# Hybrid linear-attention decode step: the gate's second product and the delta heads' decode update as float32r in row blocks of 32, another evacuation order for q and k, and packed last stores

## The chip, the cores and the metric

The kernel runs on one core of a Trainium2 chip. The metric is device time in microseconds (us): 997.32 us is the median of three runs (997.32, 997.32, 997.81). Five engines work side by side, each in its own order: PE (TensorE: matmuls; its weight loads are listed apart as PEld), DVE (VectorE), ACT (ScalarE), POOL (GpSimd) and SP, which here only issues DMAs. PE's granted clock was 0.997 of full speed in the profiled execution.

## The reference, cut to what matters

1024 prompt tokens and 8 x 8 sample tokens (T = 1088 in all) pass one layer, whose mixer has two linear-attention branches.

```python
proj = rms_norm(x) @ w_in         # q_a k_a v_a g_a z_a | qkv_b a_b b_b z_b | gate_a gate_b
# branch a (GLA, 4 heads of 64): a key-wise decay of low rank (16), from g_a
gk = log_sigmoid(g_a @ w_gla_gate + b_gla_gate) / 16
# S_t = diag(exp(gk_t)) S_{t-1} + k_t^T v_t ;  o_t = q_t S_t
# branch b (gated DeltaNet, 4 heads of 128): conv, SiLU, L2-normalised q and k, then
# S_t = exp(g_t)(I - beta_t k_t k_t^T) S_{t-1} + beta_t k_t v_t^T ;  o_t = q_t S_t
# in chunks: the inverse of (I + strict_lower(beta k k^T * gamma)) gives v_new, and
s = s * d_c + k_c^T @ v_new
# both branches: rms_norm(o) * silu(z) @ w_up, merged by sigmoid gates, @ w_out, residual,
# per-layer embedding gated by sigmoid(h @ w_ple_gate), final rms_norm
```

The outputs are y for all tokens and the new states, for the prompt and for each of the 8 sample sequences. All inputs and outputs are float32.

## The kernel before

Tokens lie along the free dimension: activations are tiles of 128 channels by tokens, in three chunks of 384, 384 and 320 tokens. PE takes a matmul of two float32 operands in two passes (two records of one instruction, such as `x2` in the timeline). The kernel avoids this nearly everywhere by splitting a float32 operand into two float32r parts, `hi` (a rounded copy, made on ACT, as `xh` from `x` or `wh` from `wr`) and `lo` (the remainder, subtracted on DVE, `xl` or `wl`), and summing three float32r products, hi·hi, hi·lo and lo·hi, in PSUM. Line 290 of the program is that product; a product of an input block over a chunk is 24 such matmuls. `w_split` (L174, L175) makes the parts of a 512 KB weight block.

*The start* is written out in order by hand: ACT, DVE, POOL and PE keep the order of the code up to `in_order.close()`. Here the first q and k blocks (`inqa`, `inka`) and half of the `v` tiles are multiplied by rows that are not normalised yet, while the row scales (`rsx`, `x_rs`) are worked out; `qk_out` then scales q and k when it evacuates them (`qa` at L385, `ka` at L391, on DVE). `x_scale` and `x_split` make the normalised `xr` and its parts for the later blocks, `x_scale` and the subtraction of `x_split` (L281) on DVE. `dup_x` copies the parts of the 64 sample tokens twice (`dupl`, `duph`) for the ninth `v` tile. 

*The recurrences* run as side tasks (generators) between the matmuls of the large input blocks. `sd.tick()` gives each a turn, and a `yield n` lets n turns pass. From the end of the written order on, a scheduler puts the instructions of each engine in order from what they need. So an edit in one task also moves instructions of others.

- `gates()` transposes the 16 gate columns `ga` of each of nine token tiles (128 columns each with zeros behind the 16) through PSUM into `gat`, evacuated on DVE (L458), and multiplies it by `wg` (16 rows of weights, zeros below) for two pairs of heads and three chunks: `gg`, L467, 6 float32 products of 128 rows. ACT and DVE turn `gg` into the running decay `b`, from which the factors `E` of the attention products `att` (L637) come.
- `gdn(h)` is the delta rule's chunked form for one head. `Gm` and `AT` are masks and products over 8 chunks. `B` holds 34 blocks of 32x32 that go through DRAM (`scra`, `scrb`), are inverted on DVE by 30 pairs of instructions `tm` (L953) and `B` (L955), and come back into `AT`; DVE transposes them into `X` (L972), and PE, ACT and DVE widen the inverses to 128 in four products (`z` L980, `x` L991 and on). Then 8 steps over the chunks (`ch`, L1034 to L1045) carry the state `S`, each passing between PE, DVE and ACT. Meanwhile the next head's convolution runs on DVE and ACT (`D`, L798).
- `gdn_sample(h)` does the same for the 64 sample tokens against 8 incoming states `S0b`. Its last step, the decode update, multiplies the keys `ktS` (32 tokens of 4 sequences at a time) by `vbb`, the new values `vn` spread over 4 sequences by a selection mask (DVE, L1122): `dSb`, L1131, two float32 products of 32 rows and 512 columns for each head. They are added to `S0b` (L1135) and stored (`out_gdn_s`, L1137). `lastpe` pins the first behind the last `ch` product so far.

*The end*: up products, output projection, the embedding's gate (`eg`, `ep`), and the final norm. The results of the last 256 tokens are made in two halves of 128 tokens and stored by four DMAs of 256 KB (`out_yT`, L1627). A partition's share of a DMA is four pieces of 128 tokens, each 512 B in DRAM.

Tiles named `half` (four slots of 128 partitions) hold, among others, `X`, `Z`, `S0b` and `vbb`; those named `small` hold `wg`, `ktS` and `vn`.

Of the kernel before, what the change touches and what calls it, by code (L numbers as in the profile page):

```python
# [104 lines left out]
def tile_hybrid_step(ctx: ExitStack, tc: tile.TileContext, xT, x0, pT, wqk, wmain, wv0, wv1, wup, wout, wpg, wpl, wgate,  # L105
                     pcols, rows, cst, sconv, sgla, sgdn,
                     yT, gla_p, gdn_p, conv_p, gla_s, gdn_s, conv_s):
    nc = tc.nc
# [40 lines left out]
    def ufree(n=1):  # L149
        sd.free_units += n  # L150
# [126 lines left out]

    def x_split(c):
        for k in range(8):
            A.copy(xh[c][:, k], xr[c][k])  # L280
            V.tensor_tensor(xl[c][:, k], xr[c][k], xh[c][:, k].bitcast(F32), op=ALU.subtract)  # L281
# [67 lines left out]
    load(rw, rows.broadcast_to([P, 8]))  # L349
    wg = [small(f"wg{hp}") for hp in range(2)]  # L350
    for hp in range(2):
        G.memset(wg[hp], 0.0)
        load(wg[hp][0:16, :], wgate[:, hp * P:(hp + 1) * P])
    K = kp.tile([P, C_K], F32, tag="K", name="K")
# [34 lines left out]
    def k_ev(hp, rs=None):  # L389
        if rs is not None:  # L390
            return lambda c, ps, o, w: V.tensor_tensor(ka[hp][:, o:o + w], ps[:, :w], rs, op=ALU.mult)  # L391
        return lambda c, ps, o, w: A.copy(ka[hp][:, o:o + w], ps[:, :w])

    def v_tiles(hf, whs, tts, dup, raw=False, lo_last=False):

        n = (272, 264)[hf]
        out = []
        for tt in tts:
# [23 lines left out]
            if hf == 0:  # L422
                A.copy(gas[tt // 4][:, (tt % 4) * P:(tt % 4) * P + 16], ps[:, 256:272])
            else:
                A.copy(ab[:, tt], ps[:, 256:264])
# [3 lines left out]
    def v_rows(tiles):  # L429
        for tt, ps in tiles:  # L430
            r = rsr[:, tt:tt + 1]
            A.mul(vr[0][tt // 4][:, (tt % 4) * 256:(tt % 4) * 256 + 256], ps[:, :256], r)
            A.mul(gas[tt // 4][:, (tt % 4) * P:(tt % 4) * P + 16], ps[:, 256:272], r)

# [12 lines left out]
    def gates():  # L447

        yield from sd.units(3)
        gat = unit("gat")  # L450
        for i in range(3):
            yield from sd.banks(1)
            n = 4 if i < 2 else 1
            ps = rps(f"gat{i}")
            for j in range(n):
                PE.transpose(ps[:, j * P:(j + 1) * P], gas[i][:, j * P:(j + 1) * P], ident)
            wd = n * P if i < 2 else NS
            V.tensor_copy(gat[:, i * 512:i * 512 + wd], ps[:, :wd])  # L458
            bfree()
            yield 5  # L460
# [409 lines left out]
    def gdn(h):  # L870
# [158 lines left out]
        for c in range(8):  # L1029
# [14 lines left out]
            mm(ps[:, 384:512], kt[:, s], vn, start=True, stop=True)  # L1044
            lastpe[h] = mm(ps[:, 0:P], Gm[:, s], vn, start=True, stop=True).ins  # L1045
            Sn = kp.tile([P, P], F32, tag="S", name=f"S{h}{c}", bufs=3)
# [40 lines left out]

    lastpe = {}

    def gdn_sample(h, kq_s, vtS, ktS, Cs, brk, sso, os_):  # L1090
# [15 lines left out]
        for b_ in range(4):  # L1106
            for c in range(4):
# [12 lines left out]
        bfree()  # L1120
        vb = half(f"vbb{h}")[lo, :512]
        V.tensor_tensor(vb.rearrange("p (b v) -> p b v", v=P), vn[lo].unsqueeze(1).broadcast_to([NS, 4, P]),  # L1122
                        sel4[lo].unsqueeze(2).broadcast_to([NS, 4, P]), op=ALU.mult)
        for g in range(2):
            V.tensor_tensor(S0v[g], S0v[g], sdec[:, h, 4 * g:4 * g + 4].unsqueeze(2).broadcast_to([P, 4, P]), op=ALU.mult)
        yield 4
        yield from sd.banks(2)
        pd = [rps(f"dSb{h}{g}") for g in range(2)]
        for g in range(2):
            r = slice(32 * g, 32 * g + 32)  # L1130
            e = mm(pd[g], ktS[r], vb[r], start=True, stop=True).ins  # L1131
            if g == 0 and h in lastpe:
                after(e, lastpe[h])
        for g in range(2):
            V.tensor_tensor(S0[g], S0[g], pd[g], op=ALU.add)  # L1135
            bfree()
# [460 lines left out]
    def normed(parts, pss, last, waits=0, ends=False):  # L1597
# [14 lines left out]
        for n, (c, r, *_) in enumerate(parts):  # L1612
            w, o, rs = r.stop - r.start, LCH[c][0] + r.start, rss[n]
            k = 4 if ends else 2
            for m0 in range(0, 8, k):
# [10 lines left out]
                yield waits  # L1626
                load(yT[m0:m0 + k, :, o:o + w].rearrange("m p w -> p m w"), yt)  # L1627

# [61 lines left out]
def _layout(i):  # L1690
# [16 lines left out]
    def vcols(m):  # L1707
# [8 lines left out]
    pcols = np.concatenate([cols(a["norm_w"]), cols(a["b_gla_gate"]), cols(a["gla_norm_w"]), cols(a["gdn_norm_w"]),  # L1716
                            cols(a["final_norm_w"]), convw], 1)
    return dict(
        xT=x.T.reshape(8, P, T), x0=x.T.reshape(8, P, T)[:, :, :384], pT=p.T.reshape(2, P, T), wqk=wqk, wmain=wmain, wv0=wv0, wv1=wv1,
        wup=np.concatenate([blocks(a["w_up_gla"][0]), blocks(a["w_up_gdn"][0])], 0)  # L1720
        .reshape(2, 2, 4, P, 4, P).transpose(0, 2, 3, 1, 4, 5).reshape(8, P, 8, P),
        wout=blocks(a["w_out"][0]), wpg=blocks(a["w_ple_gate"][0]), wpl=wpl, wgate=a["w_gla_gate"][0], pcols=pcols,
        rows=np.concatenate([a["gdn_a_log"], a["gdn_dt_bias"]], 1), cst=_consts(),
# [5 lines left out]

_OUTS = [("yT", (8, P, T)), ("gla_p", (2, P, P)), ("gdn_p", (4, P, P)), ("conv_p", (P, 12, 3)),  # L1730
         ("gla_s", (2, P, 8, P)), ("gdn_s", (4, P, 8, P)), ("conv_s", (P, 12, 24))]


def _results(g):
    y = g["yT"].reshape(1024, T).T
    return (
# [27 lines left out]
```

## Time and profile before

| | us |
|---|---|
| median of 3 runs | 997.32 |
| the profiled execution | 997.55 |
| its span (first to last instruction) | 995.4 |
| PE busy | 982.9 |
| weight load busy (beside PE) | 951.4 |
| DVE busy | 650.9 |
| ACT busy | 413.2 |
| POOL busy | 64.0 |

A row of the timeline holds the start in us from the beginning of the span, the duration in us (of all in the row), the engine, the line, the operation, `out<-in` by the program's names, the shapes, the count, and in brackets the idle time ahead of it with what ended it. Matmuls are pipelined and their ends are modelled, so starts are compared and not durations. A row of waits reads: who waited, `<-` for what, us in total, times, longest.

### The profile page before, as it was taken

What the parts mean: (1) busy time and instruction counts of PE and PEld (TensorE: products, weight loads), DVE (VectorE), ACT (ScalarE), POOL (GpSimd) and SP (SyncE); (2) the same over time, 40 slices, a digit from 0 to 9 for tenths busy, and PEclk for the clock granted to TensorE, in tenths of its full rate; (3) what the DMA queues carried; (4) which work ended last, traced back from release to release, by engine and by line L of the source; (5) the groups of instructions that cost most, each with busy time, mean ns of one, the idle gap of its engine ahead of it and who ended that gap; (6) DMA issues with size and microseconds to landing.
All of it is one profiled execution on the core that took longest, in us unless ns stands there. A gap on an engine that the chain in (4) does not pass through costs nothing.

```text
span 995.4 us, 17705 instructions
## 1 busy us (share of the span) xinstructions
PE 982.9 (99%) x6968; PEld 951.4 (96%) x6968; DVE 650.9 (65%) x1457; ACT 413.2 (42%) x989; POOL 64.0 (6%) x83
## 2 busy tenths in 40 slices
PE   9999999999999999999999999999999999999996
PEld 8999999999999989989999999999999999999996
DVE  6885745333847959866876785558777855853356
ACT  7764634432534524452264223235222222733354
POOL 0000011000000000010001000000000143200000
PEclk9999999999999999999999999999999999999998
DMA  8011112232222031313132222114442433421024
GB/s 315 15 43 64 49 57 72 77 88 72 96 73 71 30 102 23 100 66 78 68 98 73 56 77 89 43 46 141 141 126 89 132 102 89 150 85 43 22 93 152
DMA packets 65243, 84.74 MB, mean 85 GB/s; under 512 B 27188, under 2 KB 51192, under 8 KB 65160
## 3 DMA queue, kind: packets, MB, share of 16 engines
q1 hardware_dynamic: 64872, 83.22, 26.9%
q8 instruction: 55, 0.90, 0.4%
q10 hardware_dynamic: 288, 0.39, 0.1%
q14 instruction: 28, 0.23, 0.1%
HBM read 65.38 MB, written 18.21 MB: 84 GB/s over the span
## 4 chain that ended last, share of the span: by engine, by line
PE 56%; DVE 2%; ACT 0%; issue 0%; DVEq 0%
PE eg L290 10%; PE py L290 10%; PE s L1473 6%; PE inzb L290 5%; PE ing L290 5%; PE ingsg L290 5%; PE ingsh L290 4%; PE ep L290 2%; PE inza L290 1%; PE sf L1478 1%; PE se L1478 1%; PE ch L1040 1%; PE ch L1044 1%; PE ch L1045 1%; PE ch L1034 0%; PE ch L1035 0%
## 5 line engine op out<-in xcount | busy, mean ns | idle before, releaser
L175 DVE TENSOR_TENSOR wl<-wr,wh 128x1024 fp32r<-128x1024 f32 x59 | 71.9, 1221 | 65.1 <-ACT wh L174 64.7
L174 ACT CAST wh<-wr 128x1024 fp32r<-128x1024 f32 x59 | 61.7, 1049 | 107.1 <-PE ing L290 25.4
L290 PE MATMUL ing<-xh,wh 128*128 128x384 f32 (+1 forms) x288 | 97.1, 337 | 0.0
L290 PE MATMUL ing<-xh,wl 128*128 128x384 f32 (+1 forms) x288 | 94.8, 329 | 0.0
L290 PE MATMUL ing<-xl,wh 128*128 128x384 f32 (+1 forms) x288 | 94.6, 328 | 0.0
L290 PE MATMUL eg<-H,wh 128*128 128x416 f32 x256 | 69.3, 352 | 0.0
L290 PE MATMUL ingsg<-xh,wh 128*128 128x384 f32 (+1 forms) x192 | 66.5, 346 | 0.0
L290 PE MATMUL ingsh<-xh,wh 128*128 128x384 f32 (+1 forms) x192 | 66.2, 345 | 0.0
L290 PE MATMUL ingsg<-xl,wh 128*128 128x384 f32 (+1 forms) x192 | 63.1, 329 | 0.0
L290 PE MATMUL ingsh<-xl,wh 128*128 128x384 f32 (+1 forms) x192 | 62.9, 328 | 0.0
L290 PE MATMUL ingsg<-xh,wl 128*128 128x384 f32 (+1 forms) x192 | 62.8, 327 | 0.0
L290 PE MATMUL ingsh<-xh,wl 128*128 128x384 f32 (+1 forms) x192 | 62.8, 327 | 0.0
L290 PEld LDWEIGHTS ing<-xh,wh 128*128 128x128 f32 x288 | 54.2, 188 | 0.9 <-issue 0.7
L290 PEld LDWEIGHTS ing<-xl,wh 128*128 128x128 f32 x288 | 54.2, 188 | 0.5 <-issue 0.5
L290 PEld LDWEIGHTS ing<-xh,wl 128*128 128x128 f32 x288 | 54.1, 188 | 0.2 <-issue 0.2
L798 DVE SCALAR_TENSOR_TENSOR D<-R,cw,D 128x1112 f32<-128x1112 f32 x36 | 49.3, 1369 | 2.4 <-ACT D L796 2.2
L290 PEld LDWEIGHTS eg<-H,wh 128*128 128x128 f32 x256 | 47.7, 188 | 0.3
L290 PE MATMUL eg<-H,wl 128*128 128x416 f32 x128 | 44.5, 348 | 0.0
L953 DVE TENSOR_TENSOR tm<-B 34x30 f32<-34x30 f32 (+14 forms) x120 | 38.2, 319 | 7.4 <-DMA B<-scra 5.3
L955 DVE TENSOR_TENSOR B<-B,tm 34x30 f32<-34x30 f32 (+14 forms) x120 | 38.2, 318 | 1.8
L290 PEld LDWEIGHTS ingsg<-xh,wh 128*128 128x128 f32 x192 | 36.2, 188 | 2.2 <-issue 1.7
L290 PEld LDWEIGHTS ingsh<-xh,wh 128*128 128x128 f32 x192 | 36.2, 188 | 1.8 <-issue 1.1
(498 smaller groups left out, 2864.8 us busy)
## 6 DMA issues: line engine op xcount, KB each, us to landing
wr<-in_wmain SPq DMA_DIRECT2D x38, 512.0 KB, 3.5
wr<-in_wpg SPq DMA_DIRECT2D x13, 512.0 KB, 3.5
wr<-in_wup SPq DMA_DIRECT2D x8, 512.0 KB, 3.5
wr<-in_wout SPq DMA_DIRECT2D x8, 512.0 KB, 3.5
gt<-gscrg SPq DMA_DIRECT2D x16, 208.0 KB, 3.1
gt<-gscrh SPq DMA_DIRECT2D x16, 208.0 KB, 3.9
x<-in_xT SPq DMA_DIRECT2D x16, 208.0 KB, 2.4
out_yT<-y SPq DMA_DIRECT2D x8, 416.0 KB, 4.2
```

Of the source, the lines that this page charges most:

```text
L174: a = A.copy(wh, wr).ins
L175: b = (eng or V).tensor_tensor(wl, wr, wh.bitcast(F32), op=ALU.subtract).ins
L290: mm(ps[:, :w], l_, r_, start=i == 0, stop=i == len(seq) - 1)
L798: V.scalar_tensor_tensor(D[:, :n], R[:, i:n + i], cw[:, 4 * ci + i:4 * ci + i + 1], D[:, :n], op0=ALU.mult, op1=ALU.add)
L953: V.tensor_tensor(tv, Bv[:, j:j + 1, j + 1:32].broadcast_to([NBLK, j, n]), Bv[:, 0:j, j:j + 1].broadcast_to([NBLK, j, n]), op=ALU.mult)
L955: V.tensor_tensor(Bv[:, 0:j, j + 1:32], Bv[:, 0:j, j + 1:32], tv, op=ALU.add)
L1040: mm(ps[:, 256:384], AT[:, s], vt[:, s], start=True, stop=True)
L1044: mm(ps[:, 384:512], kt[:, s], vn, start=True, stop=True)
L1045: lastpe[h] = mm(ps[:, 0:P], Gm[:, s], vn, start=True, stop=True).ins
L1473: mm(ps, a[p_][:, k], Mp[b][k][q_], start=(k, i) == (0, 0), stop=(k, i) == (3, 2))
L1478: mm(ps, a[p_][:, k], M2[q_][:, k0 + k], start=first and (k, i) == (0, 0), stop=not first and (k, i) == (3, 2))
```

## The change

1. **The gate's second product.** Each 16 columns of `ga` are written four times, at 0, 32, 64 and 96, so that after the transposition the 16 rows stand in each of four row blocks of 32. ACT evacuates them as float32r, and DVE subtracts in rows 64 to 127, so that these hold the `lo` part. The weights are laid out likewise by the host (four blocks of 32 rows, 64 KB for each pair of heads rather than 8) and their blocks 1 and 3 become `lo`. One float32r product of 128 rows then sums hi·hi, hi·lo, lo·hi and lo·lo.
2. **The decode update.** A tile `kv` takes three row blocks of 32: keys as hi, hi and lo beside values as hi, lo and hi, made by 8 casts (ACT) and 4 subtractions (DVE) for each head. `vbb` is made twice, over 96 rows, and `dSb` is one float32r product of 96 rows for each half, one PSUM bank at a time. The pin `lastpe` is gone. The `half` tiles of a head are eight rather than six, in the same four slots.
3. **q and k ahead of x.** `x_split(1)` is cut in two, and the row scales and the evacuation of the third chunk's q and k stand ahead of its last three steps.
4. **Packed last results.** The four last stores go to an output of their own, `y2`, in which each partition's share (2 KB) is contiguous; the host puts it in place.

```diff
+    def gate_cols(tt):
+        return gas[tt // 4][:, (tt % 4) * P:(tt % 4) * P + P].rearrange("p (r n) -> p r n", n=32)[:, :, 0:16]
...
-                A.copy(gas[tt // 4][:, (tt % 4) * P:(tt % 4) * P + 16], ps[:, 256:272])
+                A.copy(gate_cols(tt), ps[:, 256:272].unsqueeze(1).broadcast_to([P, 4, 16]))
...
-        gat = unit("gat")
+        gat = unit("gat", F32R)
...
-            V.tensor_copy(gat[:, i * 512:i * 512 + wd], ps[:, :wd])
+            A.copy(gat[:, i * 512:i * 512 + wd], ps[:, :wd])
+            g_ = gat[NS:, i * 512:i * 512 + wd]
+            V.tensor_tensor(g_, ps[NS:, :wd], g_.bitcast(F32), op=ALU.subtract)
...
-            lastpe[h] = mm(ps[:, 0:P], Gm[:, s], vn, start=True, stop=True).ins
+            mm(ps[:, 0:P], Gm[:, s], vn, start=True, stop=True)
...
-        vb = half(f"vbb{h}")[lo, :512]
-        V.tensor_tensor(vb.rearrange("p (b v) -> p b v", v=P), vn[lo].unsqueeze(1).broadcast_to([NS, 4, P]),
-                        sel4[lo].unsqueeze(2).broadcast_to([NS, 4, P]), op=ALU.mult)
...
-        yield 4
-        yield from sd.banks(2)
-        pd = [rps(f"dSb{h}{g}") for g in range(2)]
+        kv = kp.tile([P, HW], F32R, tag="half", name=f"kv{h}", bufs=4)
+        kr, vr_ = (kv[:, o:o + 256].rearrange("p (g n) -> p g n", n=P) for o in (0, 256))
+        blk = [slice(32 * i, 32 * i + 32) for i in range(3)]
         for g in range(2):
-            r = slice(32 * g, 32 * g + 32)
-            e = mm(pd[g], ktS[r], vb[r], start=True, stop=True).ins
-            if g == 0 and h in lastpe:
-                after(e, lastpe[h])
+            me, other = blk[g], blk[1 - g]
+            for r in blk[:2]:
+                A.copy(kr[r, g], ktS[me])
+            for r in (me, blk[2]):
+                A.copy(vr_[r, g], vn[me])
+            V.tensor_tensor(kr[blk[2], g], ktS[me], kr[me, g].bitcast(F32), op=ALU.subtract)
+            V.tensor_tensor(vr_[other, g], vn[me], vr_[me, g].bitcast(F32), op=ALU.subtract)
+        yield 3
+        R3 = slice(0, 96)
         for g in range(2):
-            V.tensor_tensor(S0[g], S0[g], pd[g], op=ALU.add)
+            vb = kp.tile([P, HW], F32R, tag="half", name=f"vbb{h}{g}", bufs=4)[R3]
+            V.tensor_tensor(vb.rearrange("p (b v) -> p b v", v=P), vr_[R3, g].bitcast(F32).unsqueeze(1).broadcast_to([96, 4, P]),
+                            sel4[R3].unsqueeze(2).broadcast_to([96, 4, P]), op=ALU.mult)
+            yield 2
+            yield from sd.banks(1)
+            pd = rps(f"dSb{h}{g}")
+            mm(pd, kr[R3, g], vb, start=True, stop=True)
+            V.tensor_tensor(S0[g], S0[g], pd, op=ALU.add)
...
-    x_split(1)
-    ufree(5)
+    x_split(1, range(5))
     x_rs(2, ps)
     qk_out(2, evs)
+    x_split(1, range(5, 8))
+    ufree(5)
...
+    for w_, r_ in zip(wg, wgr):
+        A.copy(w_, r_)
+        for r in (slice(32, 64), slice(96, 128)):
+            V.tensor_tensor(w_[r], r_[r], w_[r].bitcast(F32), op=ALU.subtract)
...
-                load(yT[m0:m0 + k, :, o:o + w].rearrange("m p w -> p m w"), yt)
+                load(y2[r.start // w][:, m0:m0 + k] if ends else yT[m0:m0 + k, :, o:o + w].rearrange("m p w -> p m w"), yt)
```

In the rows below the word ahead of each is its line in the program, and the lines of the change are some 7 to 24 higher. The number behind a name tells apart tiles of one name.

The first place is DVE in the written order of the start, before: the scaling of the second chunk's x ends (`xl_388`), then q and k of the third chunk are evacuated.

```order
L281 TENSOR_TENSOR xl_388<-xr_118,xh_387 128x384 x2
L281 TENSOR_TENSOR xl_388<-xr_120,xh_387 128x384 x2
L281 TENSOR_TENSOR xl_388<-xr_122,xh_387 128x384 x2
L281 TENSOR_TENSOR xl_388<-xr_124,xh_387 128x384 x2
L385 SCALAR_TENSOR_TENSOR qa_193<-inqa_2_613,rsx_236 128x320
L391 TENSOR_TENSOR ka_194<-inka_2_638,rsx_236 128x320
L276 SCALAR_TENSOR_TENSOR xr_126<-xr_126,pc,rsx_236 128x320 x3
```

The same place after the change:

```order
L281 TENSOR_TENSOR xl_388<-xr_118,xh_387 128x384 x2
L281 TENSOR_TENSOR xl_388<-xr_120,xh_387 128x384 x2
L281 TENSOR_TENSOR xl_388<-xr_122,xh_387 128x384
L385 SCALAR_TENSOR_TENSOR qa_193<-inqa_2_613,rsx_236 128x320
L391 TENSOR_TENSOR ka_194<-inka_2_638,rsx_236 128x320
L281 TENSOR_TENSOR xl_388<-xr_122,xh_387 128x384
L281 TENSOR_TENSOR xl_388<-xr_124,xh_387 128x384 x2
L276 SCALAR_TENSOR_TENSOR xr_126<-xr_126,pc,rsx_236 128x320 x3
```

The two evacuations have moved ahead of three subtractions; nothing else has moved there.

The second place is PE in head 0's chunk steps, before: the pair of updates stands right behind the products of a `ch` step.

```order
L1040 MATMUL ch_4347<-R_3461,AT_2778 128x128
L290 MATMUL ing_0_4455<-xh_197,wl 128x384
L290 MATMUL ing_0_4455<-xh_197,wh 128x384
L290 MATMUL ing_0_4455<-xl_198,wh 128x384
L290 MATMUL ing_0_4455<-xh_197,wl 128x384
L1044 MATMUL ch_4347<-vn_4370,R_2627 128x128
L1045 MATMUL ch_4347<-vn_4370,Gm_2777 128x128
L1131 MATMUL dSb_4399<-vbb_4299,ktS_3052 128x512
L1131 MATMUL dSb_4400<-vbb_4299,ktS_3052 128x512
L1034 MATMUL ch_4415<-S_4387,D_2772 128x128
L1035 MATMUL ch_4415<-S_4387,D_2884 128x128
```

After the change, from the next step's first products on:

```order
L1041 MATMUL ch_4429<-S_4409,D_2781 128x128
L1042 MATMUL ch_4429<-S_4409,D_2893 128x128
L1150 MATMUL dSb_4444<-vbb_4398,kv_4310 128x512
L290 MATMUL ing_1_4527<-xl_388,wh 128x384
L290 MATMUL ing_1_4527<-xh_387,wl 128x384
L290 MATMUL ing_1_4527<-xh_387,wh 128x384
L290 MATMUL ing_1_4527<-xl_388,wh 128x384
L1047 MATMUL ch_4429<-R_3470,AT_2787 128x128
```

The first update stands behind the next step's first two products, alone between them and an in-block; the second follows 15 rows later, behind that step's last product and two in-block rows.

The third place is DVE at the end of head 1's inversion, before (rows of `B` and `tm` with other work between):

```order
L955 TENSOR_TENSOR B_3941<-B_3941,tm 34x26x5
L953 TENSOR_TENSOR tm<-B_3941 34x108
L955 TENSOR_TENSOR B_3941<-B_3941,tm 34x27x4
L953 TENSOR_TENSOR tm<-B_3941 34x84
L955 TENSOR_TENSOR B_3941<-B_3941,tm 34x28x3
L953 TENSOR_TENSOR tm<-B_3941 34x58
L955 TENSOR_TENSOR B_3941<-B_3941,tm 34x29x2
L175 TENSOR_TENSOR wl<-wr,wh 128x1024
```

After the change:

```order
L805 SCALAR_TENSOR_TENSOR D_4604<-R_4466,cw,D_4604 128x1112
L960 TENSOR_TENSOR tm<-B_3950 34x84
L805 SCALAR_TENSOR_TENSOR D_4604<-R_4466,cw,D_4604 128x1112
L962 TENSOR_TENSOR B_3950<-B_3950,tm 34x28x3
L805 SCALAR_TENSOR_TENSOR D_4604<-R_4466,cw,D_4604 128x1112
L960 TENSOR_TENSOR tm<-B_3950 34x58
L890 SCALAR_TENSOR_TENSOR Gm_4609<-Gm_4609,dcum,K 128x128
L962 TENSOR_TENSOR B_3950<-B_3950,tm 34x29x2
L890 SCALAR_TENSOR_TENSOR Gm_4609<-Gm_4609,dcum,K 128x128
L960 TENSOR_TENSOR tm<-B_3950 34x30
L890 SCALAR_TENSOR_TENSOR Gm_4609<-Gm_4609,dcum,K 128x128
L962 TENSOR_TENSOR B_3950<-B_3950,tm 34x30
```

Three convolution steps and three mask rows of the next head have come in between the last steps of the inversion, which before had them behind it. The rows that follow, up to the transposition into `X`:

```order
L890 SCALAR_TENSOR_TENSOR Gm_4609<-Gm_4609,dcum,K 128x128 x4
L894 SCALAR_TENSOR_TENSOR Gm_4609<-Gm_4609,dcum,K 64x64
L1085 TENSOR_SCALAR os_4022<-os_4022,rsto_4509 128x128
L175 TENSOR_TENSOR wl<-wr,wh 128x1024
L979 STREAM_TRANSPOSE X_4534<-AT_3498 32x8x32
```

Before, the weight split `wl` that stands here ahead of `X` stood behind it. And on PE the first of the sixteen pairs `z` of this head stood behind 14 matmuls of `ing_2`; now it stands behind all 24 of them and behind 15 of `ingsg_0`.

More of the change, by code (lines that the diff above doesn't have):

```diff
@@ L106, in tile_hybrid_step @@
                      pcols, rows, cst, sconv, sgla, sgdn,
-                     yT, gla_p, gdn_p, conv_p, gla_s, gdn_s, conv_s):
+                     yT, y2, gla_p, gdn_p, conv_p, gla_s, gdn_s, conv_s):
     nc = tc.nc
@@ L276, in x_scale, with x_split @@
             V.scalar_tensor_tensor(xr[c][k], xr[c][k], pc[:, V_NW + k:V_NW + k + 1], xs[c], op0=ALU.mult, op1=ALU.mult)
-    def x_split(c):
-        for k in range(8):
+    def x_split(c, ks=range(8)):
+        for k in ks:
             A.copy(xh[c][:, k], xr[c][k])
@@ L349, in tile_hybrid_step @@
     load(rw, rows.broadcast_to([P, 8]))
-    wg = [small(f"wg{hp}") for hp in range(2)]
+    wgr = [small(f"wgr{hp}") for hp in range(2)]
+    wg = [kp.tile([P, P], F32R, tag="sm", name=f"wg{hp}", bufs=13) for hp in range(2)]
     for hp in range(2):
-        G.memset(wg[hp], 0.0)
-        load(wg[hp][0:16, :], wgate[:, hp * P:(hp + 1) * P])
+        load(wgr[hp], wgate[:, hp * P:(hp + 1) * P])
     K = kp.tile([P, C_K], F32, tag="K", name="K")
@@ L432, in v_rows @@
             A.mul(vr[0][tt // 4][:, (tt % 4) * 256:(tt % 4) * 256 + 256], ps[:, :256], r)
-            A.mul(gas[tt // 4][:, (tt % 4) * P:(tt % 4) * P + 16], ps[:, 256:272], r)
+            A.mul(gate_cols(tt), ps[:, 256:272].unsqueeze(1).broadcast_to([P, 4, 16]), r)
     def dup_x():
@@ L1086, in gdn @@
         done.add(f"ob{h}")
-    lastpe = {}
     def gdn_sample(h, kq_s, vtS, ktS, Cs, brk, sso, os_):
@@ L1717, in _layout @@
                             cols(a["final_norm_w"]), convw], 1)
+    wgate = np.zeros((4, 32, 256), np.float32)
+    wgate[:, :16] = a["w_gla_gate"][0]
+    wgate = wgate.reshape(P, 256)
     return dict(
@@ L1721, in _layout @@
         .reshape(2, 2, 4, P, 4, P).transpose(0, 2, 3, 1, 4, 5).reshape(8, P, 8, P),
-        wout=blocks(a["w_out"][0]), wpg=blocks(a["w_ple_gate"][0]), wpl=wpl, wgate=a["w_gla_gate"][0], pcols=pcols,
+        wout=blocks(a["w_out"][0]), wpg=blocks(a["w_ple_gate"][0]), wpl=wpl, wgate=wgate, pcols=pcols,
         rows=np.concatenate([a["gdn_a_log"], a["gdn_dt_bias"]], 1), cst=_consts(),
@@ L1727, in _layout @@
     )
-_OUTS = [("yT", (8, P, T)), ("gla_p", (2, P, P)), ("gdn_p", (4, P, P)), ("conv_p", (P, 12, 3)),
+_OUTS = [("yT", (8, P, T - 256)), ("y2", (2, P, 8, P)), ("gla_p", (2, P, P)), ("gdn_p", (4, P, P)), ("conv_p", (P, 12, 3)),
          ("gla_s", (2, P, 8, P)), ("gdn_s", (4, P, 8, P)), ("conv_s", (P, 12, 24))]
 def _results(g):
-    y = g["yT"].reshape(1024, T).T
+    y = np.concatenate([g["yT"].reshape(1024, T - 256).T, g["y2"].transpose(0, 3, 2, 1).reshape(256, 1024)], 0)
     return (
```

## Prediction

> **What bounds the kernel now.** I read the totals of the page first, then the list of what TensorE (PE) waited for.
>
> ```profile
> span 995.4 us, 17705 instructions
> PE 982.9 (99%) x6968; PEld 951.4 (96%) x6968; DVE 650.9 (65%) x1457; ACT 413.2 (42%) x989; POOL 64.0 (6%) x83
> ...
> PE ssy L1655 <- DVE es L1654: 1.3, 2, 1.0
> PE z L980 <- DVE X L972: 1.3, 1, 1.3
> ...
> PE v L406 <- DVE qa L385: 0.7, 1, 0.7
> ```
>
> PE is busy for 982.9 of 995.4 us. What is left is the start, the end behind the last product, and a handful of waits of about 1 us. So an edit is worth what it takes from PE's own stream of instructions, plus what it takes from one of those waits, plus what it takes from the end. DVE's 65% is a mean over stages: in two of them, below, it is nearly full, and there DVE's place in the order matters.
>
> **The gate's product.** The timeline of PE around two of the six products `gg`, each run as two passes (x2):
>
> ```profile
> 92.91 0.81 PE L467 MATMUL gg<-gat,wg 128*128 128x384 f32 x2
> ...
> 93.72 0.33 PE L290 MATMUL inqa<-xl,wh 128*128 128x384 f32 x1
> 93.89 0.33 PE L290 MATMUL inqa<-xh,wl 128*128 128x384 f32 x1
> ...
> 96.28 0.70 PE L467 MATMUL gg<-gat,wg 128*128 128x320 f32 x2
> ...
> 96.99 0.33 PE L290 MATMUL inqa<-xl,wh 128*128 128x384 f32 x1
> ...
> L467 PE MATMUL gg<-gat,wg x12: 430/484/486, 92.9 to 104.0; 128*128 128x384 f32 x8, 128*128 128x320 f32 x4
> ```
>
> Matmuls overlap in the records, so their price is the distance of their starts. A float32r product of 384 columns costs 93.89 - 93.72 = 0.17. From 92.91 to 93.72 there are `gg` and one such product, so `gg` costs 0.81 - 0.17 = 0.64. As one float32r product with the same 128 rows it costs 0.17: 0.47 less, four times. With 320 columns it costs 0.71 - 0.17 = 0.54 now and 0.15 then (the rows 426.44 and 426.59 below): 0.39 less, twice. Together **-2.65**. This is the safest term, since the new instruction has the very form of the in-blocks beside it.
>
> What is paid for it lies on ACT and DVE: `gat` is evacuated on ACT, DVE subtracts over 64 rows where it copied 128, and the weights take two casts and four small subtractions. The first consumer for which this could matter is the first attention product:
>
> ```profile
> 113.81 0.43 DVE L625 TENSOR_TENSOR E<-E,qa 128x256 f32<-128x256 f32 x1
> ...
> 116.16 1.16 PE L637 MATMUL att<-E 64*128 64x128 f32 x16
> ```
>
> Its factor is ready at 114.24, 1.9 us ahead of 116.16. PE arrives 2.65 earlier. DVE, which gets from `gg` to `E` with hardly a gap, gains little from faster products, perhaps 0.4. So 2.65 - 0.4 - 1.9 = **+0.4** comes back. Bounds: 0 if the whole chain moves along, 1.5 if DVE's added work of about 1 us delays it.
>
> **The decode update.** The trace has a stretch with a pair `dSb` and one without, both behind the same `ch` products:
>
> ```profile
> 382.17 0.39 PE L1045 MATMUL ch<-vn,Gm 128*128 128x128 f32 x2
> ...
> 382.57 0.34 PE L290 MATMUL inza<-xh,wl 128*128 128x384 f32 x1
> ...
> 481.75 0.39 PE L1045 MATMUL ch<-vn,Gm 128*128 128x128 f32 x2
> 482.07 1.13 PE L1131 MATMUL dSb<-vbb,ktS 32*128 32x512 f32 x4
> 483.38 0.31 PE L290 MATMUL ingsh<-xl,wh 128*128 128x320 f32 x1
> ...
> L1131 PE MATMUL dSb<-vbb,ktS x16: 587/640/692, 401.5 to 660.4; 32*128 32x512 f32 x16
> ...
> 983.46 0.28 PE L290 MATMUL eg<-H2h,wh 128*128 128x256 f32 x1
> 983.58 0.28 PE L290 MATMUL eg<-H2l,wh 128*128 128x256 f32 x1
> ```
>
> 481.75 to 483.38 is 1.63, 382.17 to 382.57 is 0.40: a pair costs 1.23, four heads 4.9. A float32r product over 96 rows and 512 columns stands nowhere in this trace. I estimate it from 0.12 at 256 columns (983.46 to 983.58) and 0.17 at 384, so 0.22 to 0.23 at 512; eight are 1.8, and the saving is **-3.1**. Bounds: at the low end nothing is hidden better than that, so -3.3; at the high end each product, standing alone between others, costs twice as much (0.45), as a change of the row form may, and -1.3 is left. I take the near end, because a product of fewer columns in the same number format is the nearest row.
>
> Each head also gets 8 casts of 32x128 on ACT, 4 subtractions on DVE and a second `vbb`. ACT is 42% busy and nobody is near waiting for it there. DVE is another matter.
>
> **Head 1's inversion.** It holds the one wait of PE in the middle of the kernel (`z`, 1.3):
>
> ```profile
> 379.33 0.68 DVE L1122 TENSOR_TENSOR vbb<-vs,K 64x512 f32<-64x512 f32 x1
> ...
> 417.00 0.20 DVE L955 TENSOR_TENSOR B<-B,tm 34x30 f32<-34x30 f32 x1
> 417.12 2.77 DVE L798 SCALAR_TENSOR_TENSOR D<-R,cw,D 128x1112 f32<-128x1112 f32 x2
> ...
> 421.36 1.40 DVE L883 SCALAR_TENSOR_TENSOR Gm<-Gm,dcum,K 128x128 f32<-128x128 f32 x5
> ...
> 424.99 0.24 PE L980 MATMUL z<-X,AT 32*32 32x32 f32 x2 [1.29 <-DVE X L972]
> ...
> 426.44 0.31 PE L290 MATMUL ing<-xl,wh 128*128 128x320 f32 x1
> 426.59 0.31 PE L290 MATMUL ing<-xh,wl 128*128 128x320 f32 x1
> ...
> 426.79 1.05 ACT L174 CAST wh<-wr 128x1024 fp32r<-128x1024 f32 x1 [1.54 <-PE ing L290]
> ...
> 427.87 1.23 DVE L175 TENSOR_TENSOR wl<-wr,wh 128x1024 fp32r<-128x1024 f32 x1 [2.00 <-ACT wh L174]
> ...
> 596.22 0.21 DVE L955 TENSOR_TENSOR B<-B,tm 34x30 f32<-34x30 f32 x1
> ...
> 600.14 0.43 DVE L972 STREAM_TRANSPOSE X<-AT 32x256 f32<-32x256 f32 x1 [2.59 <-DMA AT<-scrb]
> ...
> 377.00:424.50 47.50, 46.57 (x300) 44.52 (x298) 44.22 (x122) 20.26 (x56) 1.86 (x1) 1.00 0.20 64
> ```
>
> The last row is busy time by engine from 377.00 to 424.50 (PE, weight load, DVE, ACT): DVE is idle for 3.3 of 47.5. In the new order DVE does, ahead of the end of `B`, four subtractions (about 0.3 each, between the 0.20 of 34x30 and the 0.68 of 64x512), one `vbb` more (0.68), three convolution steps (1.39 each) and three mask rows (0.28 each) that stood behind it: 1.2 + 0.7 + 4.2 + 0.8 = 6.9. Some of the idle time is used up, so I take 5.4: `B` ends at 422.6 and not 417.2 (times here are before's, with what was saved ahead of head 0 left out for all engines alike). From the end of `B` at 596.43 to `X` at 600.14 another head needs 3.7 for the DMAs. So `X` could start at 426.3.
>
> PE would have reached `z` at 424.99 - 1.29 = 423.7. In the new order ten in-block products of 0.15 and fifteen of 0.17 come ahead of it, and head 0's update is 0.8 cheaper: 423.7 + 1.5 + 2.6 - 0.8 = 427.0. But a weight split (`wl`) now stands on DVE ahead of `X`, and its cast starts when PE has finished with `ing`, fifteen products earlier, at 424.4. Cast 1.05, split 1.2, transpose 0.43: 427.2 or 427.3. Both paths end within half a microsecond, PE waits some 0.3 there, and two further transposes may cost another 0.5. So 0.8 replaces 1.3: **-0.5**. Bounds: -1.3 (nothing waits), and +2.5 (none of DVE's idle time is used, and DVE waits on the head-0 chain for 2 us more). Heads 2 and 3 have 8 us and more between `X` and `z`, and head 0's inversion keeps its order.
>
> **q and k evacuated earlier.** This takes away the 0.7 of `v <- qa`, if something else isn't late right behind it. The row of the stretch from 50.00 to 69.50 shows DVE busy for 19.43 of 19.50, so bringing two rows forward only pushes the others back:
>
> ```profile
> 50.00:69.50 19.50, 18.81 (x151) 18.41 (x150) 19.43 (x42) 13.06 (x30) 0.31 (x1) 1.00 0.18 55
> ...
> 69.32 1.14 ACT L440 CAST dupl<-xl 128x512 fp32r<-128x512 f32 x2 [1.58 <-DVE xl L281]
> ...
> 70.89 0.35 PE L406 MATMUL v<-wvh,duph 128*128 128x272 f32 x1
> ```
>
> The last of DVE's `xl` releases ACT's `dupl`, and behind those come the evacuations that `v` needs, at 70.89. The sum of DVE's work up to there is unchanged, so PE stops there for what it no longer loses at `qa`. I count **-0.05** (0 to -0.7).
>
> **The end.** The last four stores are 256 KB each. The rows: their issues, the time of the last one to landing, the queue's packets, megabytes and share of 16 engines over 989.2 to 994.5, and for comparison the same for two stores of `out_gdn_s` from 661.5 to 665.4:
>
> ```profile
> 989.33 2.37 SPq L1627 DMA_DIRECT2D out_yT<-y  x4
> ...
> DMA to landing us min/median/max: 3.0/3.0/3.0
> ...
> q1 hardware_dynamic: 2112, 1.05, 66.1%
> ...
> q1 hardware_dynamic: 288, 0.52, 35.2%
> ```
>
> The old pieces are 512 B: 0.661 x 5.3 us x 16 engines over 2112 packets are 26.5 ns each, 106 ns for 2 KB. The other stores move 2 KB pieces: 0.352 x 3.9 x 16 / 256 = 86 ns. 106 to 86 shortens 3.5 us of transfer to 2.84, **-0.7**. Bounds: 0 if the last landing hangs on its own latency, -0.9 if the larger pieces save a quarter of the 3.5 us. The Trainium skill, "DMA: Bandwidth & Descriptors", Specifications, says that transfers of at least 512 B already run at line rate. By that rule the packing would bring nothing and the sum would be 0.7 less favourable; the row of 86 against 106 ns speaks against it, though it is of another tensor.
>
> Elsewhere: the larger gate weights (128 KB in all) are loaded with the first inputs and needed at 92.91, and one `out_gdn_s` per head is issued later on SP, behind a weight load that is early anyway.
>
> **Sum.** -2.65 + 0.4 - 3.1 - 0.5 - 0.05 - 0.7 = -6.6. The profiled execution took 997.55 us (2.15 lie outside the span), which is 0.23 above the median of 997.32. 997.32 - 6.6 = **990.7**.
>
> **The rivals.** *DVE takes it back*: around heads 0 and 1 DVE is 93% busy (44.22 of 47.50), and the `ch` chain, on which PE's order rests, runs through it. With 1.9 us added per head and no slack, two heads give back 3.7: 994.4. The 3.3 us of idle time and the fact that PE waited for DVE only 1.3 us there speak against it. *The end gains nothing*, because each store is bound by its latency or by bytes and not by packets: 991.4. *The new update costs what it does at worst* (0.45 each): 992.5. For it speaks that the trace has no row of 96 rows, against it that every float32r row it has follows its columns. *q and k gain their full 0.7*, if `v` at 70.89 isn't held: 990.0; DVE's 19.43 of 19.50 speaks against it. *Slower than before*: `B` of head 1 ends so late that PE stands at `z`. Each microsecond beyond 422.9 (where `X` by the DMA's 3.7 meets PE) costs one. 6.6 + 2 are used up when `B` ends at 431.5, 14 us later than now, twice what I added up: 999.3 and more. For it speaks that DVE runs in order, so that one late `ch` product holds the whole of `B` behind it; against it that this wait of PE is 1.3 us in all now, and that PE passes the `ch` products sooner, not later. *The change doesn't do what it says*, say the update still in two passes, is the price of 0.45 again.
>
> **How the numbers follow.** Forecast 0.52, DVE takes it back 0.20, the end 0.13, the dear update 0.05, q and k 0.06, slower 0.04. A measurement of this kernel can tell about 0.2%, 2 us, from no change. All but the second and the last are faster by more than that; of the second I put 0.12 there and 0.08 within 2 us. That gives faster 0.88, same 0.08, slower 0.04. The range goes from 988.6 (the update at its best, no wait at `z`, q and k in full, partly together) to 994.5, which takes in the other cases but the worse part of the second and the last.
>
> **What would show it.** `gg` as single records at 0.17 or 0.15 distance; `dSb` as 8 records of 96 rows, and the time from the product ahead to the one behind some 0.25 more than without. In PE's waits: no `v <- qa`, but one of like size at the ninth `v` tile, `z` at 0.3 to 0.8, a new `att` of about 0.4. At the end: the last landing 2.3 us after its issue and not 3.0. I am wrong if PE's waits grow by more than 2 us, or if `dSb` takes 0.4 and more.

## The result, and the profile after

The changed kernel takes 990.37 us (median of 6 runs, 989.80 to 991.49) against 997.68 before (6 runs beside them): a ratio of 0.9929, 95% interval 0.9916 to 0.9942. That is 7.3 us less where 6.6 were forecast, and 990.37 where 990.7 stood. That the times agree more closely than the savings is chance: the forecast started from 997.32, 0.36 below the median of the six. The profiled run of the change is the slowest of its six, 991.49 with a span of 989.7. From its page and its list of what PE waited for, and below them one row of the same list before:

```profile
span 989.7 us, 17732 instructions
...
PE 978.0 (99%) x6954; PEld 949.0 (96%) x6954; DVE 658.0 (66%) x1481; ACT 421.5 (43%) x1026; POOL 63.8 (6%) x81
...
PE ssy L1676 <- DVE es L1675: 1.3, 2, 1.0
PE v L410 <- ACT ab L429: 1.0, 1, 1.0
PE z L987 <- DVE cvp L801: 0.8, 1, 0.8
PE ch L1047 <- ACT qs L1045: 0.4, 1, 0.4
```

```profile
PE ch L1040 <- ACT qs L1038: 0.7, 2, 0.4
```

Two of PE's waits are as foretold: `v <- qa` is gone and a wait of like size stands at the ninth `v` tile (`v <- ab`, 1.0), and `z` costs 0.8 and not 1.3. The new wait of about 0.4 at `att` is not there. The forecast had passed over the waits at `ch`: it called `z` the one wait in the middle of the kernel and said that nobody is near waiting for ACT there. Before there were two, of 0.35 each, in the steps of heads 1 and 2; now there is one of 0.35, in those of head 0. The timeline around a gate product of each size, around two update products among float32r products, and around one behind a float32 product:

```profile
94.30 0.33 PE L474 MATMUL gg<-gat,wg 128*128 128x384 f32 x1
94.47 0.34 PE L290 MATMUL inqa<-xh,wh 128*128 128x384 f32 x1
...
96.72 0.31 PE L474 MATMUL gg<-gat,wg 128*128 128x320 f32 x1
96.87 0.34 PE L290 MATMUL inqa<-xh,wh 128*128 128x384 f32 x1
...
482.11 0.40 PE L1150 MATMUL dSb<-vbb,kv 96*128 96x512 f32 x1
482.35 0.33 PE L290 MATMUL ing<-xh,wh 128*128 128x384 f32 x1
...
657.55 0.46 PE L1047 MATMUL ch<-R,AT 128*128 128x128 f32 x2
657.76 0.47 PE L1150 MATMUL dSb<-vbb,kv 96*128 96x512 f32 x1
658.08 0.34 PE L290 MATMUL inzb<-xh,wh 128*128 128x384 f32 x1
```

By the distance of starts `gg` now costs 0.17 and 0.15, as forecast to the hundredth. For `dSb` this distance is 0.24 in six of its eight places and 0.32 in the two behind a `ch` product, where 0.23 was the estimate. But an in-block product directly behind a float32 one has a longer distance too, and the rows around head 0's first update show that `dSb` only takes that over from the in-block product behind it. First without an update (before), then with one (the change):

```profile
382.17 0.39 PE L1045 MATMUL ch<-vn,Gm 128*128 128x128 f32 x2
382.31 0.42 PE L290 MATMUL inza<-xl,wh 128*128 128x384 f32 x1
382.57 0.34 PE L290 MATMUL inza<-xh,wl 128*128 128x384 f32 x1
```

```profile
402.68 0.39 PE L1042 MATMUL ch<-S,D 128*128 128x128 f32 x2
402.82 0.48 PE L1150 MATMUL dSb<-vbb,kv 96*128 96x512 f32 x1
403.14 0.34 PE L290 MATMUL ing<-xl,wh 128*128 128x384 f32 x1
403.32 0.33 PE L290 MATMUL ing<-xh,wl 128*128 128x384 f32 x1
```

From `ch` to the second in-block product is 0.40 without and 0.64 with the update, so it costs 0.24 here too: the in-block product at 382.31 has 0.26 behind the float32 one, that at 403.14 only 0.18. At the end of the program the queue's row over 983 to 988.5 and the last store's time to landing:

```profile
q1 hardware_dynamic: 576, 1.05, 49.4%
...
DMA to landing us min/median/max: 2.2/2.2/2.2
```

The last landing takes 2.2 us where it took 3.0, and 0.494 x 5.5 x 16 / (576 - 64 small ones) is 85 ns for each packet of 2 KB, against 106 for four of 512 B.

### The profile page after: what moved, and what is told of

Its sections match the earlier page's. It is cut to its first block, busy times and chain, and to the rows that moved or that the text cites. A ratio compares the mean times of both kernels' runs of the same rounds, so it can differ in the third digit from the quotient of the medians.

```text
span 989.7 us, 17732 instructions
## 1 busy us (share of the span) xinstructions
PE 978.0 (99%) x6954; PEld 949.0 (96%) x6954; DVE 658.0 (66%) x1481; ACT 421.5 (43%) x1026; POOL 63.8 (6%) x81
## 4 chain that ended last, share of the span: by engine, by line
PE 56%; DVE 0%; ACT 0%; DVEq 0%; issue 0%
PE py L290 10%; PE eg L290 10%; PE s L1494 6%; PE inzb L290 5%; PE ing L290 5%; PE ingsg L290 5%; PE ingsh L290 4%; PE ep L290 2%; PE inza L290 1%; PE se L1499 1%; PE sf L1499 1%; PE ch L1047 1%; PE ch L1051 1%; PE ch L1052 1%; PE ch L1041 0%; PE ch L1042 0%
```

## The experiments

Before's own time in the three groups of experiments was 997.53, 997.57 and 997.75. My theory was the forecast's sum, term by term; the rivals were those of the forecast. The first four kernels each make one part of the change alone.

**The gate alone** (edit: the parts of the diff on `gate_cols`, `gat`, `wg` and the host's layout).

> The gate's second product alone as float32r; update, q/k order and stores as before. My theory: gg falls from 0.64 to 0.17 us (384 columns) and from 0.54 to 0.15 (320), 2.65 us in all, and at the first att product up to 0.4 comes back because the factor E moves less than PE does: 997.7 - 2.3 to 2.65 = 995.0 to 995.4, with a wait of PE at att of 0 to 0.4. Rival (DVE's and ACT's added work around 70 to 115 us delays the factors): the wait at att is 1 us or more and the time 996.0 or above.

Measured: 994.51 (994.28 to 995.32), ratio 0.9972, interval 0.9961 to 0.9984. From the first `gg` to the first `att` the timeline has 92.97 to 113.55 where before has 92.91 to 116.16, so 2.67 less, and nothing of it comes back at `att`:

```profile
112.98 0.42 DVE L632 TENSOR_TENSOR E<-E,qa 128x256 f32<-128x256 f32 x1
...
113.55 1.16 PE L644 MATMUL att<-E 64*128 64x128 f32 x16
```

`E` ends at 113.40, 0.15 us ahead of PE. Counted from the first `gg`, this `E` ends after 20.43 us where before it took 21.33, so DVE's chain gained 0.90 and not 0.4, which just suffices; why it gained so much was not looked into. The time is 0.5 below the low end of the expectation: nothing came back at `att`, and 0.35 us went outside the span (last section). A later wait at `z` of head 0 took 0.2 back in this kernel, but not in the whole change.

**The decode update alone** (edit: the parts on `gdn_sample` and `lastpe`).

> The decode update alone as float32r products of 96 rows, with its tiles, without the pin. My theory: each dSb costs 0.23 rather than 0.62, 3.1 us in all, and PE's wait at z of head 1 goes from 1.3 to 0.8: 997.7 - 3.6 = 994.1. Rival A (a product of 96 rows between others of 128 costs 0.45): 997.7 - 1.3 - 0.5 = 995.9. Rival B (DVE takes it back in the ch chain): dSb at 0.23, but PE's waits at ch and z grow by 2 us and more, 996 or above.

Measured: 993.75 (992.91 to 994.32), ratio 0.9962, interval 0.9949 to 0.9974. The products cost 0.24, PE's waits at `z` are 0.8 and at `ch` 0.4. My theory's 994.1 stands, both rivals fall. Of the 3.8 us, 0.35 lie outside the span and are no part of the theory.

**q and k alone** (edit: the parts on `x_split`).

> Only the third chunk's q and k evacuated ahead of the last three steps of x_split(1). My theory: the wait v <- qa of 0.7 goes, and a wait of like size stands at the ninth v tile, since DVE is busy for 19.43 of 19.50 us there: 997.7 - 0.05, within 0.3 of before. Rival (v is not held there): 997.0. Rival (ACT's x casts come later and v's evacuations with them): 998.2.

Measured: 996.82 (996.52 to 997.35), ratio 0.9994, interval 0.9986 to 1.0003: no difference that can be told, though the median is 0.7 lower, which by itself fits the first rival (997.0) better than my theory's 0.3. Half of the 0.7 lies outside the span (last section). The wait moved as my theory says, and was not shortened:

```profile
PE v L406 <- ACT ab L425: 0.9, 1, 0.9
```

**The packed stores alone** (edit: the parts on `y2`).

> Only the last four stores to the packed output, 2 KB pieces rather than 512 B. My theory: the last store lands 2.1 to 2.4 us after its issue rather than 3.0, and the time from the last PE product to the end of the span falls from 7.41 by 0.7: 997.0. Rival (512 B already run at line rate, the end is a matter of bytes or latency): landing stays at 3.0 and the time at 997.7.

Measured: 996.99 (996.61 to 997.65), ratio 0.9996, interval 0.9987 to 1.0005. By time alone it can't be told from none; the profile can. The last store lands 2.6 us after its issue, not within my 2.1 to 2.4, and from the last `ssy` at 987.79 to the end of the span at 994.8 are 7.01 us, 0.40 less than before's 7.41, where I expected 0.7. In the whole change it is 6.81 (982.89 to 989.7). The rest of that gain isn't shown to be the packing's: the gate alone, whose stores are the old ones, also ends sooner, 7.11 us behind its last `ssy` (985.69 to 992.8). The last `ssy` and the queue's row over the end (986.9 to 992.2, 988.9 to 994.3) of the gate alone, then of the packed stores alone:

```profile
985.69 0.49 PE L1666 MATMUL ssy<-es,ones 128*128 128x128 f32 x2 [0.30 <-DVE es L1665]
...
q1 hardware_dynamic: 2112, 1.05, 65.9%
...
987.79 0.49 PE L1655 MATMUL ssy<-es,ones 128*128 128x128 f32 x2 [0.30 <-DVE es L1654]
...
q1 hardware_dynamic: 576, 1.05, 50.9%
```

By the way of counting used above a 2 KB packet takes 86 ns in the packed stores alone, and four of 512 B take 106 in the gate alone, as before. So the 0.30 of the gate alone comes from something else than the time of a packet; what it is was not found.

The four medians are 3.0, 3.8, 0.7 and 0.5 below before's, 8.05 in all, and the whole change gives 7.3: the 0.35 outside the span is in three of the four, and only once in the whole.

**Why the first profile of the change was its slowest run.** In it the first `gg` stands at 94.30, 1.4 us later than before, though nothing of the change runs ahead of it on PE. On ACT in the first 25 us:

```profile
23.07 0.20 ACT L501 ACTIVATE nea<-rw 128x4 f32<-128x4 f32 x1 [2.83 <-DMA rw<-in_rows]
23.19 0.56 ACT L261 ACTIVATE rsx<-ssx,eps_t 128x384 f32<-128x384 f32 x1
```

Before had `nea` at 20.80 and `rsx` at 21.88. `nea` needs 8 numbers (`rw`) that are loaded behind all of x; nobody needs its result for long, but ACT takes its instructions in order, so the row scales `rsx` of the first chunk stand behind it. Before, `rsx` waited for PE's `ssx` instead; in the change `ssx` came only 0.14 later and would have let `rsx` start at about 22.0. If that is what moves, an earlier load of `rw` should cure it. The second group tried this:

```diff
+    rw = kp.tile([P, 8], F32, tag="rw", name="rw")
     for c in (1, 2):
         for _ in x_load(c):
             pass
-    rw = kp.tile([P, 8], F32, tag="rw", name="rw")
-    load(rw, rows.broadcast_to([P, 8]))
+        if c == 1:
+            load(rw, rows.broadcast_to([P, 8]))
```

> The changed kernel with one load moved: the 8 numbers a row of rw are fetched between the second and the third chunk of x rather than behind both. My theory: in the profile of the change ACT stood at nea for rw until 23.07 us, the row scales of the first chunk came behind it, DVE's work to 70 us followed, and PE paid 1.4 us at the ninth v tile. With rw early nea runs before the row scales are due, ACT's first rsx starts on PE's ssx at about 21.4, v <- duph at 70.5 to 70.9, the time is 989.4 to 989.9 and the runs lie closer together. Rival (the late DMAs of x themselves are the cause, rw only shares their fate): rsx still starts at 22 and above in some runs, and the time is that of the change run again.

> The changed kernel again, as the partner of the others here. My theory: 990.4, between 989.8 and 991.5, with nea ending anywhere between 20.7 and 23.3 us and the ninth v tile between 70.8 and 72.4 accordingly (38.7 us behind DVE's first scaling of x).

> The changed kernel with rw early and with q and k evacuated behind x_split(1) as before. My theory: DVE sets the ninth v tile either way (38.6 to 38.8 us from its first scaling of x to v <- duph), so this is within 0.2 of the changed kernel with rw early; v <- qa stands in PE's waits with 0.7 to 1.3 and v <- ab does not. Rival (the early q and k are worth 0.7, as their median alone, 996.8 against 997.5, says): this is slower by 0.5 to 0.7.

> The kernel before with rw early. My theory: its ACT was held by rw only now and then (nea at 20.80 in the first profile, ahead of ssx), so the median falls by 0 to 0.5 from 997.5, and the upper runs around 998 go. The difference of the changed kernel to before, both with rw early, is then 7.3 to 7.8. Rival: the same time and spread as before.

Measured, in this order: 997.72 (996.76 to 998.71), 990.03 (989.82 to 990.45), 997.68 (996.08 to 1000.80) and 1005.08 (1003.99 to 1005.66). The cure made it 7.7 us worse with the change, and 7.5 without it (1005.08 against 997.57). ACT and PE in the first of them:

```profile
18.09 0.20 ACT L502 ACTIVATE nea<-rw 128x4 f32<-128x4 f32 x1 [7.59 <-DMA rw<-in_rows]
...
19.33 0.59 PE L411 MATMUL v<-wvh,xh 128*128 128x272 f32 x1 [4.80 <-ACT wvh L174]
19.72 0.43 PE L412 MATMUL v<-wvh,xl 128*128 128x272 f32 x1
19.95 0.43 PE L411 MATMUL v<-wvh,xh 128*128 128x272 f32 x1
```

The scheduler now puts `nea` on ACT ahead of the casts `wvh` of the weights for `v`, presumably because it counts on the load earlier. The load was issued at 9.34 behind four loads of x (1.6 MB) on the same queue and used at 18.09; for 7.6 us ACT stood, and PE waited 4.8 us for `wvh`. That is not all that PE lost. In windows of 2 us its granted clock was 1.00 up to 16 us, 0.74, then 0.50 from 18 to 22, 0.56, and 1.00 again from 24 on; the change run again has 1.00 in each of these windows. The first 24 products of `v` took 5.10 us (19.33 to 24.43, starts 0.23 apart), against 3.01 there (14.06 to 17.07, 0.125 apart). They began 5.27 later and took 2.09 longer, and this is the 7.37 by which the ninth `v` tile below is late. My expectation was wrong in its sign, since it counted the load's place and not the place of the instruction that waits for it. What the four show is the start, from these starts in the timelines (`rsx` of the first chunk on ACT, the first `xr` of the first chunk on DVE, the first product of the ninth `v` tile on PE):

| kernel | nea | rsx | xr | v tile 9 | xr to v |
|---|---|---|---|---|---|
| before | 20.80 | 21.88 | 32.25 | 70.89 | 38.64 |
| update alone | 22.63 | 22.74 | 33.09 | 71.72 | 38.63 |
| q, k alone | 22.07 | 22.18 | 32.54 | 71.14 | 38.60 |
| before, rw early | 18.16 | 28.36 | 38.74 | 77.39 | 38.65 |
| gate alone | 21.62 | 21.73 | 32.20 | 70.97 | 38.77 |
| the change | 23.07 | 23.19 | 33.65 | 72.37 | 38.72 |
| the change again | 21.11 | 21.47 | 31.96 | 70.69 | 38.73 |
| the change, rw early | 18.09 | 28.84 | 39.33 | 78.06 | 38.73 |
| the same without q, k | 19.55 | 30.05 | 40.54 | 79.30 | 38.76 |

From `rsx` on everything is fixed in these nine, however the inputs arrive: 10.4 to 10.5 us to `xr`, and 38.6 to 38.8 to the ninth `v` tile. q and k evacuated earlier take 0.03 or 0.04 off this (38.64 to 38.60, 38.76 to 38.73); the gate's part adds 0.1 (its copies of `ga` on ACT are wider; that they are the cause was not tried). The times agree, 997.72 with q and k earlier and 997.68 without, but with runs that lie 2.0 and 4.7 apart they could hardly tell 0.7. So by the profiles the q and k term is next to nothing; the 0.4 by which the median span of q and k alone is lower (995.0 after 995.4) stays unexplained. In the first profile of the change `rsx` starts 1.2 later than its `ssx` would have let it, out of the 1.5 by which the ninth `v` tile is late: that much is the arrival of `rw`. This is read from the trace; no run here takes away that wait and nothing else.

**The third group** tried two improvements and the order by itself. In `e9_rows_first` the load of `rw` stands ahead of the two loads of `v` weights; in `e12_pool` one weight split of the start is subtracted on POOL; `e10_rows_pool` has both; `e11_no_pin` is the kernel before without the pin `lastpe`.

```diff
+    rw = kp.tile([P, 8], F32, tag="rw", name="rw")
+    load(rw, rows.broadcast_to([P, 8]))
     w_load(True)
     w_load(True)
...
     w_split(V)
-    w_split(V)
+    w_split(G)
     x_split(1, range(5))
...
-            e = mm(pd[g], ktS[r], vb[r], start=True, stop=True).ins
-            if g == 0 and h in lastpe:
-                after(e, lastpe[h])
+            mm(pd[g], ktS[r], vb[r], start=True, stop=True)
```

> The changed kernel with the load of rw ahead of the v weights, so that it lands with the first chunk and ACT's nea, which the order of ACT now puts ahead of the casts wvh, waits for nothing. The moves in the last call put rw behind 1.6 MB of x and ACT stood 7 to 8 us. My theory: nea ends at about 12, the first rsx starts on ssx at 21.3 to 21.5, v <- duph at 70.4 to 70.8 and the time is 989.7 to 990.0 with a spread under 0.7. Rival (the late arrival of x itself sets the start): 990.0 to 990.4 and the spread of 1.7 of the first six runs.

> The changed kernel with one wvl (128x1056, 1.2 us on DVE at about 57) subtracted on POOL. DVE sets the ninth v tile, 38.7 us behind its first scaling of x, and q and k earlier or later change nothing in that sum; taking work out of it should. My theory: the distance falls to 37.5 to 37.9, PE's wait v <- ab of 0.9 goes, time 990.0 - 0.9 = 989.1. Rival (PE's or ACT's own order holds v there): the distance stays at 38.7 or PE's wait moves to another tile, 990.0.

> Both of the last two together: rw ahead of the v weights and one wvl on POOL. My theory: 988.9 to 989.1, and the runs closer together than those of the changed kernel. Rival: no better than the better of the two.

> The kernel before without the pin lastpe, nothing else: the update's float32 products stay as they are, and the order around them moves. My theory: the format carries the gain, not the order: a pair still costs 1.2 and the time is 997.2 to 997.7. Rival (a good part of the update's 3.8 us comes from its new place in PE's order): 996.5 or less.

Measured: 990.89 (990.47 to 991.11), 991.04 (990.96 to 992.65), 993.82 (991.75 to 994.34) and 998.89 (998.23 to 1000.64; ratio 1.0013, interval 1.0004 to 1.0021). None beats the change, and my theory missed in all four; of the rivals only that of `e10_rows_pool` came. With `rw` first, `nea` waits for nothing, but the cast `wvh` came at 13.57 rather than 12.27 (in the change run again), and PE's product `ssx` and with it `rsx` came 1.3 later: what ACT no longer waits for at 21 it waits for at 13. On POOL the subtraction took far longer than the 1.2 us on DVE (a span on POOL is rough, PE's wait for it is not):

```profile
54.23 6.86 POOL L175 TENSOR_TENSOR wvl<-wr,wvh 128x1056 fp32r<-128x1056 f32 x1 [51.80 <-PE ssx L254]
...
59.53 2.91 DVE L281 TENSOR_TENSOR xl<-xr,xh 128x384 fp32r<-128x384 f32 x3
...
PE v L413 <- POOL wvl L175: 2.2, 1, 2.2
```

PE waited 2.2 us for it, and DVE's three subtractions beside it took 2.91 where they take 1.49 in the change. The distance from `xr` to `v` grew to 40.07. With both moves `rsx` starts at 23.21 and the distance is 41.59; why both together lose more than their sum was not looked into.

Without the pin the update's old products lose 1.1 us, and the timeline of head 3 says why. Before first, then without the pin:

```profile
659.85 1.13 PE L1131 MATMUL dSb<-vbb,ktS 32*128 32x512 f32 x4
660.91 0.45 PE L290 MATMUL inzb<-xh,wl 128*128 128x384 f32 x1
```

```profile
659.39 1.12 PE L1131 MATMUL dSb<-vbb,ktS 32*128 32x512 f32 x2
660.44 0.49 PE L1044 MATMUL ch<-vn,R 128*128 128x128 f32 x2
...
661.09 1.12 PE L1131 MATMUL dSb<-vbb,ktS 32*128 32x512 f32 x2
662.14 0.45 PE L290 MATMUL inzb<-xh,wh 128*128 128x384 f32 x1
```

Two products of 32 rows side by side (four records) take 1.06; one alone takes 1.05. They lie in different blocks of rows, and by these times they run at once. The pin had kept this pair together; the pairs of the other three heads stayed together without it. The Trainium skill, "TensorEngine Tiling (Array Packing)", Key Properties, says that tiles of the array work independently and can run matmuls in parallel; the trace agrees, with 1.06 for two against 1.05 for one. So leaving out the pin gains nothing with the old products, and my theory's time was 1.2 too low mostly because the old form depends on the order: by an estimate from these rows, eight old products taken apart would cost 8.4 us rather than some 4.8, while the new ones stand alone at 0.24. The order did gain elsewhere in the change, at `z` and at `ch` (below).

## Why the forecast held, step by step

The change run again had a start like before's, 0.3 earlier by chance. Its timeline (profiled at 989.82, span 988.0) against the first profile of before, cut at rows that both have, gives the terms:

| stretch | before | the change again | difference |
|---|---|---|---|
| start to the first `gg` | 92.91 | 92.63 | -0.28 |
| to the first `att` | 23.25 | 20.58 | -2.67 |
| to head 0's first `z` | 239.99 | 240.00 | +0.01 |
| to the first up product `py` | 327.25 | 323.39 | -3.86 |
| to the last `ssy` | 304.59 | 304.64 | +0.05 |
| to the end of the span | 7.41 | 6.76 | -0.65 |
| outside the span | 2.15 | 1.82 | -0.33 |

The sum is -7.7, the difference of the two profiled times. Of the 1.1 by which it beats the forecast's 6.6, 0.4 is the give-back at `att` that did not come; most of the rest (0.3 at the start, 0.35 at `ch`, 0.33 outside the span) was in no term of the forecast, and that it came out on this side is luck; the update brought 0.3 less.

- *The gate*, -2.65 by its products: -2.67. Right. *Its give-back at `att`*, +0.4: none. This is the step that was mis-sized: DVE's chain from `gg` to `E` became 0.90 shorter where 0.4 was allowed for, and PE met `E` with 0.15 us to spare.
- *The update*, -3.1: about -2.8. Eight products at 0.24 make 1.9 where 1.8 was estimated; the bound of 0.45 was far off. The larger miss is in the old pairs: 1.23 was measured at head 1 and taken for all four, but head 0's pair stood between float32 products and cost 1.05 (401.16 to 402.53 before is 1.37, with 0.32 for the `ch` ahead of it). The four cost about 4.8 and not 4.9.
- *Head 1's inversion*, -0.5: from 1.29 to 0.75, -0.54. The mechanism was the second of the two paths that were named, the weight split ahead of `X` (rows of the first profile of the change):

```profile
424.17 1.03 ACT L174 CAST wh<-wr 128x1024 fp32r<-128x1024 f32 x1
...
425.24 1.22 DVE L175 TENSOR_TENSOR wl<-wr,wh 128x1024 fp32r<-128x1024 f32 x1 [1.39 <-ACT wh L174]
426.38 0.42 DVE L979 STREAM_TRANSPOSE X<-AT 32x256 f32<-32x256 f32 x1
...
426.86 0.24 PE L987 MATMUL z<-X,AT 32*32 32x32 f32 x2 [0.75 <-DVE cvp L801]
```

  The list names `cvp`, the last of DVE's instructions to finish ahead of `z`; what held it is the chain `wh`, `wl`, `X` above it. The whole wait lies at the first `z`, where 0.3 was foretold, and none at the later transposes, where 0.5 was. The cast did not start when PE let go of the weights but behind ACT's exponentials of `Gm`, which is why it was later there.
- *The waits at `ch`* were not in the sum: two of 0.35 went with the new order and one of 0.35 came. With the two above this makes 3.7 of the 3.86.
- *q and k*, -0.05: -0.03 to -0.04 by the starts. Right, and for the reason given.
- *The end*, -0.7: -0.65. The size is right, the reason only in part: the packing by itself gave 0.40, with 85 or 86 ns against 106 for 2 KB, and the gate alone, whose packets took as long as before, gave 0.30 that no term of the forecast has. The rule of the Trainium skill ("DMA: Bandwidth & Descriptors", Specifications) that 512 B already run at line rate doesn't hold for these stores: 106 ns for 2 KB in pieces of 512 B, 85 in one.
- *Outside the span*, not in the sum: about 0.35. See the last section.

The rival that DVE takes it back did not come, but not because DVE's idle time took up the added work: DVE is busy for 44.22 of 47.50 us in this stretch in both (377.00 to 424.50 before, 374.05 to 421.55 in the change run again). The last steps of the inversion came later instead, and PE's waits from head 0 to the up products went from 2.0 to 1.1. The rival on the slower side needed `B` of head 1 to end 14 us later than before in the same place; it ended at 419.24 in the change run again (2.0 us later than before's 417.20, or some 5.0 us once the 2.9 saved ahead are added, where the prediction took 5.4).

## What to carry to other kernels

A product on a full engine is worth what its starts say: compare the distance with and without it in the same stretch, and look at every place: the gate's term, whose places are alike, held to 0.02 us, while the update's missed by 0.3, in part because one pair was priced for all four. Where an engine is busy from end to end, bringing one of its instructions forward gained 0.03 or 0.04 us here; count what lies between its first input and its last result instead. And before a load is moved, look where the instruction that waits for it will stand in its engine's order: here a small load moved forward held ACT for 7.6 us where it had held it for 1.4 to 3.0, and PE lost another 2.1 us by its lower clock behind the wait.

## What the runs showed of the hardware that was not expected

- Two float32 products of 32 rows in different row blocks overlap fully (1.06 us for the pair, 1.05 for one alone); the one pair that was split apart cost twice as much.
- A float32r product of 96 rows and 512 columns costs 0.24 us among float32r products of 128 rows. Its distance is 0.32 directly behind a float32 product, where an in-block product of 384 columns has 0.26 rather than 0.17.
- In the change with `rw` early PE stood for 4.8 us, and its granted clock fell to 0.50 and was 1.00 again from 24 us on; the 24 products behind the wait took 5.10 us rather than 3.01.
- A subtraction of 128x1056 on POOL took 6.86 us beside a busy DVE, and 1.2 on DVE, where POOL's spans are rough; POOL's subtractions of 128x512 late in the kernel take 1.3.
- The time outside the span is 2.1 to 2.3 us in all runs of before, of the packed stores alone, and of the kernels that only move `rw` or drop the pin, and about 1.8 in nearly all runs of the kernels with the gate's, the update's or the q and k part. It goes with the program and not with its work, and half of the 0.7 us by which the median of q and k alone seemed to fall is this. Its cause was not found.
